# Two pairs of heads in one run of products with V, the compressed branch in the same run, gate rows through DRAM, and earlier loads of the compression weights

## The chip, the core and the metric

The kernel runs on one core of one Trainium2 chip. The metric is the device time of one execution in microseconds (us), as the median of several runs.

## The reference, cut to what is computed

Two transformer blocks of two layers each (DEPTH 2) act one after the other on x of 256 tokens by 1024. In the first block a context stream of another 256 tokens runs beside x in layer 0. Each of its layers, cut:

```
px = split_cols(hx @ w_in);  pc = split_cols(hc @ w_in)
ya, yca = global_gqa(...)             # 8 heads, "A"
yb, ycb = neighbourhood_attn(...)     # 8 heads, "B"
yc_, ycc = window_gqa(...)            # 8 heads, "C"
ux = concat([ya, yb, yc_]) * silu(px[9])
x = x + gate[:, None, :] * (ux @ w_out)
if need_ctx:                          # layer 0 alone
    uc = concat([yca, ycb, ycc]) * silu(pc[9])
    cx = cx + gate_c * (uc @ w_out)
```

`gate` and `gate_c` are rows of 1024 numbers, the last third of `c_silu @ ada_w + ada_b`. Each layer of the second block, cut:

```
x = x + 0.5 * swiglu(rms(x, ffn1_norm), ffn1_wg, ffn1_wu, ffn1_wd)
y_a = nsa(...) @ w_branch_nsa         # compressed + selected + window, 8 heads, "N"
y_b = moba(...) @ w_branch_moba       # 8 heads, "M"
x = x + (sigmoid(ga) * y_a + sigmoid(gb) * y_b) @ w_out
x = x + 0.5 * swiglu(rms(x, ffn2_norm), ffn2_wg, ffn2_wu, ffn2_wd)
```

In `nsa` the keys and values are also compressed (a two-layer net with weights w1 and w2 over blocks of 32 tokens), and each query attends to those few compressed keys too (`o_cmp = p_cmp @ vcb`); the three results are added with a gate per head.

## The kernel before

All large weights lie in one packed DRAM array and come in as tiles of up to 128x1024 f32 on SP's queue (`ws`, `_dma`, L260), in the fixed order of a plan. Each is split for TensorE by a cast on ScalarE into `wh` (L286) and a subtraction on VectorE into `wl` (L287), two tiles ahead of its use. `gemm` makes three products for each block of rows (`three`, L426 to L428: hi·hi, hi·lo, lo·hi) and adds them in a bank of PSUM (`acc`).

Beside the gemms run lanes: Python generators for the preparation of Q, K and V and for attention. After each block of gemm products `q()` gives the lanes a budget of time and `step()` takes the next step of the lane that lies furthest back. So the order of the program is that of Python; a scheduling layer then sets the order on each engine by what is ready.

`attention` handles units (a head, or half of one) of one or two slots. In each slot: scores (`f_s`, L514 and L515), softmax (`f_m`, L550; `f_n`, L566 to L574), transposes by TensorE of the normalised weights (`f_t`, L580, bank `pst`), a copy out (`f_e`, L596 or L598) to a tile `pt` in SBUF, of which there are three. `f_v` (L609) makes the products with V for two units: the stationary V is 64 columns wide, one unit fills the upper 64 partitions of the bank `pso`, the other the lower. A product of f32 operands shows in the trace as two records, called passes below. `evac` then adds the bank to its place (L985, L988) or splits it (L1398, L1412). `f_v` comes as soon as both units have ended one slot earlier. In the heads N a closure `extra` (L1374) adds the compressed branch to the bank: products 128 columns wide whose operands `Vb` and `pcT` fill 64 partitions.

At the end of a layer of block 1 the lanes are drained and the attention pools closed (L1097, L1098); then `gate` (tile `gt`) takes their space. For each stream and half row, four products with a broadcast column of `mod` and the identity (L1116) put the gate row on all partitions in a bank `psx`, and VectorE copies it (L1117). `w_out` runs on; `add` multiplies its banks by `gt` (`tmp`, L1123) and adds to x (L1124). In layer 0 the tile x had been overwritten by its normalised form at the start and then used for silu(gate) columns, so x and ctx are loaded again at L1110; `uc`, the context's input of `w_out`, is split at L1107 and L1108.

In block 2 the attention stage `mix` begins (L1205, L1218) by loading w1 (two tiles of 128x16x128, 1 MB each, in packets of 512 bytes) and w2 on ScalarE's queue, into tiles `big0`, `big1` and `w2` of the stage's own pools.

Of the kernel before, what the change touches and what calls it, by code (L numbers as in the profile page):

```python
# [228 lines left out]
class Body:  # L229
# [272 lines left out]
    def attention(self, units, evac):  # L502
# [97 lines left out]
        def f_v(x):  # L600
            pair = units[x:x + 2]
            O = self.ps("o")[:, :2 * P]
            extra = pair[1].get("extra")
            nk = len(pair[0]["v"])
            for k in range(nk):
                for i in (1, 0):
                    u = pair[i]
                    v, b, m, c = u["v"][k]
                    nc.tensor.matmul(O[HD * i:HD * i + HD, c:c + m * P], v, u["pt"][:, b:b + m, :].rearrange("p m t -> p (m t)"),  # L609
                                     start=k == 0, stop=k == nk - 1 and extra is None)  # L610
            if extra is not None:
                extra(O)
            evac(O, pair[1])

# [12 lines left out]
        for s in range(n):  # L627
# [11 lines left out]
            while nv < len(units) and ends[nv + 1] < s:  # L639
                f_v(nv)  # L640
                c += 430 * len(units[nv]["v"])
                nv += 2
            yield c
        while nv < len(units):
            f_v(nv)
            nv += 2
            yield 430.0
# [108 lines left out]
    def ada_close(self, g):  # L756
# [12 lines left out]
        while b < nb:  # L769
# [4 lines left out]
            for s in range(2):  # L774
# [5 lines left out]
                if a < z:  # L780
                    nc.vector.scalar_tensor_tensor(self.mod[l][:, s, a:z], self.mod[l][:, s, a:z], 1.0,
                                                   self.col("norm_w", 8 * l + a - 8, z - a), op0=ALU.add, op1=ALU.mult)
            b = e

# [35 lines left out]
    def block1(self, x):  # L820
        nc, tc = self.nc, self.tc
        cx = self.cx1
        with ExitStack() as es:
            hp = es.enter_context(tc.tile_pool(reuse_waits="tile", name="hT", bufs=1))
            hT = self.new_hT(hp, 0)
            with tc.tile_pool(reuse_waits="tile", name="w0", bufs=START_TILES) as self.w0:
                self.start(x, cx, hT)
# [5 lines left out]
    def start(self, x, cx, hT):  # L833
# [9 lines left out]
        self.norm_rows(x, x)  # L843
        self.norm_rows(cx, cx)

        def half(h):
            for c in (4 * h, 4 * h + 2):
                for s, v in enumerate((x, cx)):
                    self.mod_pair(0, s, c, self.turn_pair(v, c), hT)
# [31 lines left out]
    def layer1(self, l, x, cx, hT, hp):  # L881
# [3 lines left out]
        with ExitStack() as lay:  # L885
            lp = lay.enter_context(tc.tile_pool(reuse_waits="tile", name=f"lay{l}", bufs=1))
            if need:
                sg2 = lp.tile([P, 4, T], F32, name="sg2")
                xv, cv = (t.rearrange("p t (a d) -> p (t a) d", d=T) for t in (x, self.cx1))

                def sg(c, n):
                    return (xv, cv, sg2)[c // 4][:, c % 4:c % 4 + n, :]
# [17 lines left out]
            sink = lp.tile([P, 8], F32, name=f"sink{l}")  # L910
# [719 lines left out]
```

## Time and profile before

| quantity | value |
|---|---|
| device time, 3 runs | 1947.4 us median (1946.05 to 1948.95) |
| the profiled execution | 1947.63 us, its span 1945.8 us |
| TensorE (PE) | 1904.4 us busy, 98% of the span; granted clock 0.992 in the mean |
| VectorE (DVE) / ScalarE (ACT) / GpSimd (POOL) | 1279.4 us (66%) / 1103.3 us (57%) / 1.0 us |
| the chain that ended last | 92% PE, of which 72% gemm products (L426 to L428), 4% products with V, 4% transposes |
| DMA | 294.62 MB, 151 GB/s in the mean |

In the rows below a line of the timeline reads: start and length in us, engine, source line, operation, output and input tiles, shape, count. What stands in square brackets is how long the engine was idle before, and what ended that. Passes overlap, so what one costs is the distance of its start to the next start. PEclk in the windows is the granted clock as a share of full speed.

### The profile page before, as it was taken

Reading aid. Unit: us, or ns where it says so; the run is one execution under the profiler, and the core shown is the slowest. Engines: PE = TensorE matmul, PEld = TensorE weight load, DVE = VectorE, ACT = ScalarE, POOL = GpSimd, SP = SyncE. Lnnn points to the kernel's source line nnn. Section 1 sums busy time; section 2 is a strip of 40 time slices with the busy share of each in tenths; the row PEclk is TensorE's granted clock in tenths of the full one; section 3 lists DMA queues with packets and bytes.
Section 4 is the critical chain, followed back from the end, with each engine's and each line's share of the span. In section 5 each row is a group of like instructions: output and inputs, shape, how many; then the busy total and the mean of one; then the engine's idle time right before and its main releaser. Section 6 shows DMA issues by size and latency. Waiting matters only on the chain.

```text
span 1945.8 us, 27694 instructions
## 1 busy us (share of the span) xinstructions
PE 1904.4 (98%) x10348; PEld 1561.0 (80%) x10348; DVE 1279.4 (66%) x2490; ACT 1103.3 (57%) x1979; POOL 1.0 (0%) x7
## 2 busy tenths in 40 slices
PE   8999999999999999999899999999999899999998
PEld 3777778777988877888788878888888788888886
DVE  5486856788596787555689575555555588675555
ACT  4367657775567675444467645445444458655443
POOL 0000000000000000000000000000000000000000
PEclk9999999999999999999999999999999999999999
DMA  7333324135422236554523565554555433456552
GB/s 304 106 123 130 118 90 150 55 131 186 136 93 95 85 109 216 184 184 141 166 93 125 164 215 198 183 191 173 193 186 173 144 106 101 152 180 234 186 181 74
DMA packets 85270, 294.62 MB, mean 151 GB/s; under 512 B 10000, under 2 KB 10384, under 8 KB 85136
## 3 DMA queue, kind: packets, MB, share of 16 engines
q1 hardware_dynamic: 80432, 283.39, 43.0%
q10 hardware_dynamic: 4704, 9.47, 1.5%
q8 instruction: 81, 1.33, 0.3%
q14 instruction: 53, 0.43, 0.1%
HBM read 291.77 MB, written 1.05 MB: 150 GB/s over the span
## 4 chain that ended last, share of the span: by engine, by line
PE 92%; DVE 4%; ACT 2%; issue 1%; ACTq 1%; DMA 1%; SPq 0%; DVEq 0%
PE acc L426 24%; PE acc L428 24%; PE acc L427 24%; PE pso L609 4%; PE pst L580 4%; PE pss L514 2%; PE pss L515 2%; PE psr L715 1%; DVE wl L287 1%; PE psx L1173 1%; ACT wh L286 1%; PE psr L721 1%; PE psm L747 1%; PE psm L1260 1%; PE acc L750 1%
## 5 line engine op out<-in xcount | busy, mean ns | idle before, releaser
L287 DVE TENSOR_TENSOR wl<-ws,wh 128x1024 fp32r<-128x1024 f32 (+2 forms) x538 | 638.1, 1188 | 478.8 <-ACT wh L286 476.0
L286 ACT CAST wh<-ws 128x1024 fp32r<-128x1024 f32 (+2 forms) x538 | 549.2, 1024 | 573.3 <-PE acc L428 503.3
L426 PE MATMUL acc<-wh,xt 128*128 128x512 f32 (+3 forms) x1120 | 419.6, 376 | 11.7 <-ACT wh L286 11.7
L427 PE MATMUL acc<-wl,xt 128*128 128x512 f32 (+3 forms) x1120 | 416.6, 372 | 0.0
L428 PE MATMUL acc<-wh,xt 128*128 128x512 f32 (+3 forms) x1120 | 416.4, 373 | 0.0
L426 PEld LDWEIGHTS acc<-wh,xt 128*128 128x128 f32 x1120 | 212.1, 190 | 44.9 <-ACT wh L286 12.9
L428 PEld LDWEIGHTS acc<-wh,xt 128*128 128x128 f32 x1120 | 211.8, 189 | 33.0 <-issue 0.7
L427 PEld LDWEIGHTS acc<-wl,xt 128*128 128x128 f32 x1120 | 212.7, 190 | 31.2 <-issue 0.3
L426 PE MATMUL acc<-wh,hT 128*128 128x384 f32 (+2 forms) x480 | 159.6, 333 | 0.1
L427 PE MATMUL acc<-wl,hT 128*128 128x384 f32 (+2 forms) x480 | 158.5, 330 | 0.0
L428 PE MATMUL acc<-wh,hT 128*128 128x384 f32 (+2 forms) x480 | 158.1, 329 | 0.0
L550 ACT ACTIVATE p<-pss,nm 128x512 f32<-128x512 f32 (+2 forms) x240 | 127.5, 539 | 20.3 <-DVE nm L546 5.1
L426 PE MATMUL acc<-wh,hffn 128*128 128x512 f32 x352 | 137.7, 391 | 0.0
L428 PE MATMUL acc<-wh,hffn 128*128 128x512 f32 x352 | 137.1, 389 | 0.0
L427 PE MATMUL acc<-wl,hffn 128*128 128x512 f32 x352 | 137.0, 389 | 0.0
L580 PE MATMUL pst<-consts,p 128*128 128x128 f32 x624 | 103.3, 278 | 0.0
L427 PEld LDWEIGHTS acc<-wl,hT 128*128 128x128 f32 x480 | 90.6, 189 | 7.2 <-issue 1.9
L426 PEld LDWEIGHTS acc<-wh,hT 128*128 128x128 f32 x480 | 90.5, 189 | 6.8 <-issue 0.8
L428 PEld LDWEIGHTS acc<-wh,hT 128*128 128x128 f32 x480 | 90.5, 189 | 5.8 <-issue 1.2
L580 PEld LDWEIGHTS pst<-consts,p 128*128 128x128 f32 x624 | 72.2, 140 | 28.5 <-ACT p L572 5.6
L572 ACT ACTIVATE p<-p,rinv 128x256 f32<-128x256 f32 (+2 forms) x152 | 81.5, 573 | 16.5 <-DVE rinv L566 12.2
L428 PEld LDWEIGHTS acc<-wh,hffn 128*128 128x128 f32 x352 | 66.1, 188 | 13.9
(318 smaller groups left out, 2868.5 us busy)
## 6 DMA issues: line engine op xcount, KB each, us to landing
ws<-in_wall SPq DMA_DIRECT2D x476, 512.0 KB, 3.4
ws<-in_wall SPq DMA_DIRECT2D x64, 384.0 KB, 3.1
bias<-in_bias ACTq DMA_DIRECT2D x8, 512.0 KB, 4.0
x<-in_x SPq DMA_DIRECT2D x2, 1024.0 KB, 6.5
cx<-in_ctx SPq DMA_DIRECT2D x2, 1024.0 KB, 10.3
ws<-in_wall SPq DMA_DIRECT2D x4, 420.0 KB, 3.0
out<-y SPq DMA_DIRECT2D x2, 512.0 KB, 2.6
ws<-in_wall SPq DMA_DIRECT2D x2, 280.0 KB, 2.8
```

What stands on the lines that cost most here:

```text
L286: self.nc.scalar.copy(h[:, :n], s[:, :n])
L287: self.nc.vector.tensor_tensor(lo[:, :n], s[:, :n], h[:, :n].bitcast(F32), op=ALU.subtract)
L426: mm(out, ah, bh, start=start, stop=False)
L427: mm(out, ah, bl, start=False, stop=False)
L428: mm(out, al, bh, start=False, stop=stop)
L514: nc.tensor.matmul(S[:, o:o + w], q, kh, start=True, stop=False)
L515: nc.tensor.matmul(S[:, o:o + w], q, kl, start=False, stop=True)
L550: nc.scalar.activation(p[:, o:o + w], S[:, o:o + w], AF.Exp, bias=nm[:, i:i + 1], accum_out=sm[:, i:i + 1])
L572: nc.scalar.activation(p[:, o:o + w], p[:, o:o + w], AF.Copy, scale=r[:, i:i + 1])
L580: nc.tensor.transpose(t[:, i * P:(i + 1) * P], sl["P"][:, o:o + P], self.ident)
L609: nc.tensor.matmul(O[HD * i:HD * i + HD, c:c + m * P], v, u["pt"][:, b:b + m, :].rearrange("p m t -> p (m t)"), start=k == 0, stop=k == nk ...
L715: nc.tensor.transpose(p[:, 2 * a + g, :], ks[:, t, a, g, :], self.ident_r)
```

## The change

Six edits:

1. `f_v(x, n)` takes n = 2 pairs (four units): their products form one run, and both results lie in one bank, 256 columns each. In the loop it is called when all four units have ended a slot earlier, once per slot; what is left follows after the last slot. There are five `pt` tiles.
2. The compressed branch becomes products 64 columns wide in that same run: `extra` is now a list of four, `Vb` and `pcT` fill 128 partitions, the tile `scmp` is padded to eight rows with zeros by GpSimd.
3. x stays in its tile: the first norm writes to `xn0`, silu(gate) columns have a tile `sg0`, and only ctx is loaded again.
4. The gate rows go through DRAM: when `mod` is finished, GpSimd's queue writes its gate columns to a DRAM tile (`gate_rows`), and at the end of the layer one broadcast DMA per stream, on ScalarE's queue, reads the row into `gt` (L1126 of the new kernel). The 24 products and 6 copies are gone.
5. `cmp_load`: w1 and w2 are issued in the second round of `ffn1` instead of at the start of `mix`, into tiles of a pool that lasts through block 2.
6. The last norm's weight is loaded one stage later; the sink values share one tile.

```diff
-                u["pt"] = self.pp.tile([P, 8, P], F32, tag="pt", name=f"pt_{self.uid}", bufs=3)
+                u["pt"] = self.pp.tile([P, 8, P], F32, tag="pt", name=f"pt_{self.uid}", bufs=5)
...
+        def f_v(x, n):
+            pairs = [(units[x + 2 * j], units[x + 2 * j + 1], 2 * P * j) for j in range(n)]
+            O = self.ps("o")
+            todo = []
+            for pair in pairs[::-1]:
+                for k in range(len(pair[0]["v"])):
+                    for i in (1, 0):
+                        v, b, m, c = pair[i]["v"][k]
+                        todo.append((i, c + pair[2], m * P, v, pair[i]["pt"][:, b:b + m, :].rearrange("p m t -> p (m t)")))
+            for pair in pairs[::-1]:
+                todo += [(i, c + pair[2], P, v, p) for i, c, v, p in pair[1].get("extra", [])]
+            for y, (i, c, w, v, p) in enumerate(todo):
+                nc.tensor.matmul(O[HD * i:HD * i + HD, c:c + w], v, p, start=y < 2, stop=y >= len(todo) - 2)
+            for pair in pairs:
+                evac(O[:, pair[2]:pair[2] + 2 * P], pair[1])
...
-            while nv < len(units) and ends[nv + 1] < s:
-                f_v(nv)
-                c += 430 * len(units[nv]["v"])
-                nv += 2
+            if nv + 3 < len(units) and ends[nv + 3] < s:
+                f_v(nv, 2)
+                c += 860 * len(units[nv]["v"])
+                nv += 4
...
+    def gate_rows(self, l, c0, n):
+        if l not in self.gates:
+            self.gates[l] = self.gp.tile([2, KD, P], F32, name=f"gates{l}")
+        c = c0 // P
+        for s in range(2 if l == 0 else 1):
+            self.nc.gpsimd.dma_start(self.gates[l][s, c:c + n // P, :].rearrange("j p -> p j"), self.mod[l][:, s, 16 + c:16 + c + n // P])
...
-                    for t, nm in ((x, "x"), (cx, "ctx")):
-                        nc.sync.dma_start(t, self.dram[nm].rearrange("o (t p) d -> p (o t) d", p=P))
+                    nc.sync.dma_start(cx, self.dram["ctx"].rearrange("o (t p) d -> p (o t) d", p=P))
                 for s in range(2 if need else 1):
-                    for ct in range(2):
-                        p = self.ps("x")
-                        for j in range(4):
-                            g = self.mod[l][:, s, 16 + 4 * ct + j:17 + 4 * ct + j]
-                            nc.tensor.matmul(p[:, j * P:(j + 1) * P], g.to_broadcast([P, P]), self.ident, start=True, stop=True)
-                        nc.vector.tensor_copy(gate[:, s, ct * 512:ct * 512 + 512], p)
+                    g = self.gates[l][s:s + 1].rearrange("s j p -> s (j p)")
+                    nc.scalar.dma_start(gate[:, s, :], g.to_broadcast([P, D]))
...
+    def cmp_load(self, l):
+        nc = self.nc
+        w1 = [self.bp.tile([P, 16, P], F32, tag=f"big{j}", name=f"w1{l}_{j}") for j in range(2)]
+        for j, nm in enumerate(("cmpk_w1_2", "cmpv_w1_2")):
+            nc.scalar.dma_start(w1[j], self.dram[nm][l].rearrange("(m p) j -> p m j", p=P))
...
+                if fi == 1 and name == "ffn1":
+                    self.cmp_load(l)
...
-                            def extra(O, t=t, b=b, pcT=pcT):
-                                for j in range(2):
-                                    nc.tensor.matmul(O[:, j * P:(j + 1) * P], Vb[:, b, 2 * j:2 * j + 2, :].rearrange("p r d -> p (r d)"),
-                                                     pcT[:, t, :], start=False, stop=j == 1)
+                            extra = [(i, j * P, Vb[:, b, 2 * j + i, :], pcT[:, t, :]) for j in range(2) for i in (1, 0)]
...
-            if i == 1:
+            if i == 2:
                 fw = bp.tile([P, D], F32, tag="xtrow", name="fw2")
```

**First place: TensorE, last runs of the heads A in layer 0.** Before, the two pairs have a run each (L609), with transposes and gemm products between them (`pso` is the bank of V's products, `pst` that of transposes, `pss` scores):

```order
1497 L580 MATMUL pst_3666<-consts,p_3597 128x128 x4
1498 L609 MATMUL pso_3678<-pt_3654,VG_584 64x256
1499 L609 MATMUL pso_3678<-pt_3593,VG_584 64x256
1500 L609 MATMUL pso_3678<-pt_3654,VG_584 64x256
1501 L609 MATMUL pso_3678<-pt_3593,VG_584 64x256
1502 L514 MATMUL pss_3750<-KTB_587,QTB_589 128x512
...
1514 L428 MATMUL acc_3690<-wh_3522,hT_1_109 128x384
1515 L609 MATMUL pso_3719<-pt_3717,VG_584 64x256
1516 L609 MATMUL pso_3719<-pt_3676,VG_584 64x256
1517 L609 MATMUL pso_3719<-pt_3717,VG_584 64x256
1518 L609 MATMUL pso_3719<-pt_3676,VG_584 64x256
1519 L580 MATMUL pst_3764<-consts,p_3744 128x128 x4
```

In the change the same eight products (L612) are one run in one bank:

```order
1525 L426 MATMUL acc_3692<-wh_3694,hT_0_110 128x384
1526 L612 MATMUL pso_3719<-pt_3717,VG_592 64x256
1527 L612 MATMUL pso_3719<-pt_3682,VG_592 64x256
1528 L612 MATMUL pso_3719<-pt_3717,VG_592 64x256
1529 L612 MATMUL pso_3719<-pt_3682,VG_592 64x256
1530 L612 MATMUL pso_3719<-pt_3660,VG_592 64x256
1531 L612 MATMUL pso_3719<-pt_3560,VG_592 64x256
1532 L612 MATMUL pso_3719<-pt_3660,VG_592 64x256
1533 L612 MATMUL pso_3719<-pt_3560,VG_592 64x256
1534 L580 MATMUL pst_3757<-consts,p_3737 128x128 x4
```

Over the whole program TensorE's order has 66 unbroken stretches of L609 and 10 of L1374 before, and 37 stretches of L612 now; the products in them are 320 and 16 before and 352 now.

**Second place: ScalarE at the start of the first `mix`, and where its loads stand now.** Before, the three loads stand between two casts of weight tiles:

```order
875 L286 CAST wh_9954<-ws_9886 128x840
876 L1205 DMA w_0_10014<-in_cmpk_w_2 128x16x128
877 L1205 DMA w_1_10015<-in_cmpv_w_2 128x16x128
878 L1218 DMA w_10034<-in_cols 128x128
879 L286 CAST wh_10038<-ws_9904 128x560
```

In the change they stand at the end of layer 1 of block 1, spread among casts, with that layer's gate row (`gt`, L1126) between them:

```order
754 L286 CAST wh_8332<-ws_8244 128x1024
755 L1160 DMA w_0_8787<-in_cmpk_w_2 128x16x128
756 L979 CAST u_0_7957<-cx_84 128x256
757 L1126 DMA gt_8329<-gates_2520 128x1024
758 L286 CAST wh_8350<-ws_8262 128x1024
759 L1160 DMA w_1_8788<-in_cmpv_w_2 128x16x128
760 L286 CAST wh_8397<-ws_8280 128x1024
```

The two w1 tiles of the second `mix` stand in the `w_out` of the first, two casts apart.

**Third place: VectorE at the end of layer 0 of block 1.** Before, a copy of a gate row (L1117) stands ahead of the first `tmp` (L1123):

```order
726 L1117 COPY gt_4740<-psx_4782 128x512
727 L287 TENSOR_TENSOR wl_4813<-ws_4477,wh_4812 128x1024
728 L1117 COPY gt_4740<-psx_4788 128x512
729 L1123 TENSOR_TENSOR tmp_4741<-acc_4141,gt_4740 128x512
730 L1123 TENSOR_TENSOR tmp_4741<-acc_4142,gt_4740 128x512
731 L1124 TENSOR_TENSOR x<-x,tmp_4741 128x512 x2
732 L287 TENSOR_TENSOR wl_4835<-ws_4540,wh_4834 128x1024
```

In the change the first `tmp` (L1132) follows the last subtraction of `uc` (L1122), and two tiles' `wl` stand behind it:

```order
713 L1122 TENSOR_TENSOR uc_4744<-cx_84,uc_4743 128x256
714 L1132 TENSOR_TENSOR tmp_4742<-acc_4244,gt_4741 128x512
715 L1132 TENSOR_TENSOR tmp_4742<-acc_4245,gt_4741 128x512
716 L287 TENSOR_TENSOR wl_4791<-ws_4537,wh_4790 128x1024
717 L1133 TENSOR_TENSOR x<-x,tmp_4742 128x512 x2
718 L287 TENSOR_TENSOR wl_4813<-ws_4623,wh_4812 128x1024
```

On ScalarE both broadcasts of that layer's gate rows stand directly behind the last cast of `uc` (L1121) and ahead of the cast to wh_4790.

## Rows read from the trace of the kernel before

**Rows 1.** The page's chain that ended last, by engine.

```profile
PE 92%; DVE 4%; ACT 2%; issue 1%; ACTq 1%; DMA 1%; SPq 0%; DVEq 0%
```

**Rows 2.** PE's timeline, heads A of layer 0: start us, length us, engine, line, operation.

```profile
342.50 1.08 PE L609 MATMUL pso<-pt,VG 128*64 128x256 f32 x8
343.51 0.66 PE L580 MATMUL pst<-consts,p 128*128 128x128 f32 x4
```

**Rows 3.** PE's timeline, end of layer 1 of block 1.

```profile
733.36 0.40 PE L426 MATMUL acc<-wh,u 128*128 128x512 f32 x1
733.68 1.95 PE L609 MATMUL pso<-pt,VB 128*64 128x256 f32 x16
735.56 0.50 PE L427 MATMUL acc<-wl,u 128*128 128x512 f32 x1
735.90 0.40 PE L428 MATMUL acc<-wh,u 128*128 128x512 f32 x1
736.14 0.40 PE L426 MATMUL acc<-wh,u 128*128 128x512 f32 x1
...
737.53 1.95 PE L1116 MATMUL psx<-consts,mod 128*128 128x128 f32 x16
739.24 0.47 PE L426 MATMUL acc<-wh,u 128*128 128x512 f32 x1
```

**Rows 4.** PE's timeline in the first mix: a run of heads M, the compressed products of heads N.

```profile
992.11 0.87 PE L609 MATMUL pso<-pt,mVY 128*64 128x256 f32 x8
...
1015.80 0.49 PE L1374 MATMUL pso<-pcT,Vb 64*128 64x128 f32 x2
1016.22 0.44 PE L580 MATMUL pst<-consts,p 128*128 128x128 f32 x2
```

**Rows 5.** ACT's timeline at the start of the first mix.

```profile
940.17 0.85 ACTq L1205 DMA_DIRECT2D w<-in_cmpk_w  x1
...
944.59 3.41 ACTq L1218 DMA_DIRECT2D w<-in_cols  x1
948.12 1.39 ACT L286 CAST wh<-ws 128x560 fp32r<-128x560 f32 x2 [6.67 <-issue]
```

**Rows 6.** PE's timeline, the first product after the loads, in the first and the second mix.

```profile
949.56 0.69 PE L426 MATMUL acc<-wh,xt 128*128 128x384 f32 x1 [4.97 <-ACT wh L286]
...
1542.27 0.97 PE L426 MATMUL acc<-wh,xt 128*128 128x384 f32 x2 [5.14 <-ACT wh L286]
```

**Rows 7.** Windows (us, busy us of PE, PEld, DVE, ACT, POOL with instructions, PEclk, DMA share, GB/s).

```profile
1340.00:1350.00 10.00, 9.71 (x44) 7.76 (x44) 7.59 (x19) 4.56 (x8) 0.00 (x0) 1.00 0.70 255
949.50:956.00 6.50, 6.44 (x32) 5.97 (x33) 5.58 (x21) 4.22 (x11) 0.00 (x0) 0.70 0.56 175
1542.00:1550.00 8.00, 7.73 (x36) 7.28 (x37) 6.40 (x22) 5.17 (x13) 0.00 (x0) 0.67 0.47 140
```

**Rows 8.** DMA issues of the whole run: queue, count, KB each, median us from issue to landing.

```profile
fw<-in_final_norm_w SPq DMA_DIRECT2D x1, 512.0 KB, 4.2
fw<-in_final_norm ACTq DMA_DIRECT2D x1, 512.0 KB, 7.1
w<-in_cols ACTq DMA_DIRECT2D x2, 64.0 KB, 7.1
```

**Rows 9.** DVE's timeline at the ends of the two layers of block 1.

```profile
449.59 1.28 DVE L1123 TENSOR_TENSOR tmp<-acc,gt 128x512 f32<-128x512 f32 x2
...
744.56 1.28 DVE L1123 TENSOR_TENSOR tmp<-acc,gt 128x512 f32<-128x512 f32 x2
```

**Rows 10.** ACT's timeline at the same two ends: the last cast of uc, the last of u.

```profile
443.34 0.40 ACT L1107 CAST uc<-cx 128x256 fp32r<-128x256 f32 x1
...
736.14 0.41 ACT L965 CAST u<-cx 128x256 fp32r<-128x256 f32 x1 [2.77 <-DVE cx L988]
```

**Rows 11.** PE's timeline at the end of layer 0, its last run with V.

```profile
440.83 0.82 PE L609 MATMUL pso<-pt,VB 128*64 128x256 f32 x6
441.58 0.50 PE L426 MATMUL acc<-wh,u 128*128 128x512 f32 x1
```

More of the change, by code (lines that the diff above doesn't have):

```diff
@@ L598, in f_e @@
                 nc.vector.tensor_copy(dst, src)
[L600 to L613, printed above, removed]
+        def f_v(x, n):
[13 more added lines that the diff above has]
+                evac(O[:, pair[2]:pair[2] + 2 * P], pair[1])
         ends, e = [], -1
@@ L825, in block1 @@
             hT = self.new_hT(hp, 0)
-            with tc.tile_pool(reuse_waits="tile", name="w0", bufs=START_TILES) as self.w0:
-                self.start(x, cx, hT)
+            with tc.tile_pool(reuse_waits="tile", name="w0", bufs=START_TILES) as self.w0, \
+                    tc.tile_pool(reuse_waits="tile", name="xn0", bufs=1) as xp:
+                self.start(x, cx, hT, xp)
             for l in range(DEPTH):
@@ L831, in block1, with start @@
                 hT = self.layer1(l, x, cx, hT, hp)
-    def start(self, x, cx, hT):
+    def start(self, x, cx, hT, xp):
         nc, tc = self.nc, self.tc
@@ L842, in start @@
         nc.vector.tensor_copy(self.ident_r, self.ident)
-        self.norm_rows(x, x)
-        self.norm_rows(cx, cx)
+        xn, cn = (xp.tile([P, 2, D], F32, name=f"xn0_{j}") for j in range(2))
+        self.norm_rows(x, xn)
+        self.norm_rows(cx, cn)
         def half(h):
             for c in (4 * h, 4 * h + 2):
-                for s, v in enumerate((x, cx)):
+                for s, v in enumerate((xn, cn)):
                     self.mod_pair(0, s, c, self.turn_pair(v, c), hT)
@@ L887, in layer1 @@
             if need:
-                sg2 = lp.tile([P, 4, T], F32, name="sg2")
-                xv, cv = (t.rearrange("p t (a d) -> p (t a) d", d=T) for t in (x, self.cx1))
+                sgs = [lp.tile([P, 4, T], F32, name="sg0"), cx.rearrange("p t (a d) -> p (t a) d", d=T),
+                       lp.tile([P, 4, T], F32, name="sg2")]
                 def sg(c, n):
-                    return (xv, cv, sg2)[c // 4][:, c % 4:c % 4 + n, :]
+                    return sgs[c // 4][:, c % 4:c % 4 + n, :]
             else:
@@ L909, in layer1 @@
             qn = lp.tile([P, 2, HD], F32, name=f"qn{l}")
-            sink = lp.tile([P, 8], F32, name=f"sink{l}")
+            sinks = lp.tile([P, 64], F32, name=f"sink{l}")
+            sink, nsink = sinks[:, :8], sinks[:, 8:16]
             nc.scalar.dma_start(qn[:, 0, :], self.row_bcast(self.dram["k_norm_a"], l * HD, HD))
@@ L913, in layer1 @@
             nc.scalar.dma_start(sink, self.row_bcast(self.dram["sink_c"], l * 8, 8))
-            nsink = lp.tile([P, 8], F32, name=f"nsink{l}")
             nc.vector.tensor_scalar(nsink, sink, -1.0, None, op0=ALU.mult)
@@ L1143, in layer1 @@
                 return hT
+    def cmp_load(self, l):
[3 more added lines that the diff above has]
+            nc.scalar.dma_start(w1[j], self.dram[nm][l].rearrange("(m p) j -> p m j", p=P))
+        w2 = self.bp.tile([P, 2, HD], F32, tag="w2", name=f"w2{l}")
+        o2 = COLS["w2"][0] + P * l
+        nc.scalar.dma_start(w2, self.dram["cols"][:, o2:o2 + P].rearrange("p (a d) -> p a d", a=2))
+        self.cmp_w = w1, w2
     def ffn(self, l, name, x, xt, ss, hooks, after):
@@ L1202, in mix @@
             toks = [(0, None), (1, None)]
-            w1 = [op.tile([P, 16, P], F32, tag=f"big{j}", name=f"w1{l}_{j}") for j in range(2)]
-            for j, nm in enumerate(("cmpk_w1_2", "cmpv_w1_2")):
-                nc.scalar.dma_start(w1[j], self.dram[nm][l].rearrange("(m p) j -> p m j", p=P))
+            w1, w2 = self.cmp_w
             oT = {k: [op.tile([P, 4, 256], F32R, name=f"o{k}{l}_{j}") for j in range(2)] for k in "NM"}
@@ L1349, in attn_lane @@
                         yield 2000.0
-                        sc = mp.tile([P, 2, 4, 16], F32, tag="scmp", name=f"scmp{l}{b}")
+                        scp = mp.tile([P, 2, 8, 16], F32, tag="scmp", name=f"scmp{l}{b}")
+                        nc.gpsimd.memset(scp, 0.0)
+                        sc = scp[:, :, :4, :]
                         st = mp.tile([P, 2, 4], F32, tag="stc", name=f"stc{l}{b}")
```

34 lines of the change are left out of this document (18 added, 16 removed).

## The prediction

> **What bounds the kernel now.** I read the chain that ended last first: 92% of the span is PE's own work [rows 1]. So nothing is won by relieving DVE or ACT; time goes only where PE has less to do, or where it stood idle or slow. Then I went through PE's timeline for two things. One is the distance from start to start around the runs with V [rows 2 to 4], which shows what such a run costs beyond its passes. The other is brackets with idle time: the two largest of the whole run are at the starts of the two mixes [rows 6], and ACT's timeline at that place says why [rows 5]. The windows give the clock there [rows 7]. Last, for the gate rows, which turn from PE work into a transfer, I read how long transfers of this size take [rows 8] and when the row is wanted [rows 9 to 11].
>
> **The sum** is made against the profiled execution, 1947.6 us, 0.2 above the median of the runs. 0.2% is about 4 us, what a measurement of this kernel can tell from no change.
>
> *Fewer runs with V: -8.7.* Sixteen passes take 1.88 us from their start to the next product's (733.68 to 735.56) [rows 3], eight take 1.01 (342.50 to 343.51) [rows 2]. So eight more passes cost 0.87, 0.109 each, and 1.01 - 0.87 = 0.14 is fixed in each run. The product ahead of the run takes 0.32 instead of 0.24 (733.36 to 733.68; 735.90 to 736.14 is an undisturbed one), the one behind it 0.34 instead of 0.24 [rows 3]. A run thus costs 0.14 + 0.08 + 0.10 = 0.32 beyond its passes. PE's order has 66 such runs before and 37 after, 29 fewer. Where transposes follow the run the price behind it is not in these rows, so the lower bound is 0.22 each (6.4 us), the upper 0.32 (9.3). I take 0.30, near the upper, since gemm products follow most runs: 29 x 0.30 = 8.7.
>
> *Compressed branch: -2.0.* Its 10 stretches go. Two passes take 0.42 (1015.80 to 1016.22) [rows 4]; the 128-row gate passes take 0.107 each (1.71 for sixteen, 737.53 to 739.24) [rows 3], so two would take 0.21 undisturbed: 0.2 x 10 = 2.0. The passes themselves come out even: 32 before at 0.107 are 3.4; after, 64 passes of half the width and 128 columns. A run of eight of which four are 128 columns long is 0.87 against 1.08 long [rows 4, 2], so such a pass is 0.05 cheaper than 0.109, about 0.056, and 64 are 3.6. If they cost 0.107 after all, it would be 3.4 us more.
>
> *Gate products: -5.3.* 24 products, 48 passes at 0.107 to 0.12: 5.1 to 5.8, two thirds of it in layer 0. The six copies on DVE cost nothing before as far as PE goes, and give nothing, save that in layer 0 they stood ahead of `tmp`.
>
> *Starts of the mixes: -13.* At the first, ACT is held by three DMA issues from 940.17 to about 948.0 [rows 5]; the casts of the next weight tiles stand behind them, so PE idles 4.97 us, at the second mix 5.14 [rows 6]. Then PE works at a granted clock of 0.70 for 6.5 us and 0.67 for 8.0 us, against 1.00 at the start of another stage [rows 7]: 6.5 x 0.30 + 8.0 x 0.33 = 4.6. With an estimated 1.5 us for smaller gaps and a lowered clock around the stall, that is 10.1 + 4.6 + 1.5 = 16.2. An ordinary stage start is not free: PE is busy 9.71 of 10.00 us there [rows 7], 0.6 lost in twenty us at the least; I leave 1.6 at each start. So 16.2 - 2 x 1.6 = 13. Bounds: 10 (only the idle goes) and 16.
>
> Where do the issues go? In the new order they stand at the end of layer 1 of block 1, and in the first mix's `w_out`, with casts between them. The first issue took 0.85 us, the third 3.41 [rows 5], with nothing between: the queue took them no faster than it drained. With casts between, each has some us to drain, and ACT runs two tiles ahead of PE. I price the new places at 0, covered by that lead; if the cover is gone, rival B.
>
> *Gate rows as transfers: +8.* The order puts the reads of layer 0 behind the last cast of `uc`. Before, the last run with V ended at 441.6 [rows 11] and that cast at 443.7 [rows 10]. The 512 KB broadcasts of the trace land after 4.2 and 7.1 us [rows 8], so the row is there 6.3 to 9.2 us after the run, with two of them at once rather later; before, `tmp` came 8.0 us after it (449.59) [rows 9]. But PE has less to do in the meantime. Behind the last run stand 31 gemm products (0.23 each, 7.1 us) until PE needs a bank that `tmp` frees, and two `wl` stand behind `tmp` on DVE. So PE idles between 0 and 4 us; I take 3.5, as the second read shares the engines with the first. In layer 1 the read stands behind the cast of `u` (736.14, ending 0.98 us after the run's end at 735.56) [rows 10, 3] and behind the first w1 tile. PE wants the row about 6.6 us after the run, before it was used 9.0 after (744.56) [rows 9]; it lands 1.0 + 4.2 at best, 1.0 + 10 behind a megabyte: 0 to 4.4, I take 3. Both waits can lower the clock for some us as the mix starts do [rows 7]; at half of that price, 1.5. Together 8, bounds 0 and 13.
>
> The Trainium skill, "DMA: Bandwidth & Descriptors", section "Queues, rings and completion order", speaks against this part: descriptors of one issuing queue are consumed in ring order on each DMA engine, so a gate row behind w1 on ScalarE's queue starts last. The trace agrees: 64 KB behind the w1 tiles took 7.1 us, as long as 512 KB elsewhere [rows 8]. By the rule alone the wait in layer 1 would be at its upper bound, the sum 1.4 us worse. The same page, section "Anatomy of one DMA", fits 2.0 us and 436 KB per us on GpSimd's queue, 3.2 us for 512 KB; no row here is that short, and by it the sum would be some 3 us better.
>
> *Without a price.* x is not loaded again: nothing in the rows waits for that load. GpSimd's memsets and the writes of `mod` are done long before they are read. Five `pt` tiles take away waits, none of which is on the chain by more than tenths.
>
> Sum: -8.7 - 2.0 - 5.3 - 13 + 8 = -21: 1926.6, less the 0.2: **1926.5 us**.
>
> **Rivals.**
> *A, the gate rows are in time.* They land at the lower bounds, and nothing is given back: 1926.5 - 8 = 1918.5. For it: 4.2 us [rows 8]. Against it: on ACT's queue the same size took 7.1.
> *B, the block on ACT's queue only moves.* The queue drains 2 MB no faster elsewhere; at the end of layer 1 and in `w_out` ACT is held again by some 7 us, casts come late, and PE idles about 5 us twice with the slow clock behind it: the 13 are given back, 1939.5. For it: from the first issue's start to the last one's end it was 7.8 us [rows 5]. Against it: casts stand between them now.
> *C, slower: the joined run is no longer there to fill a gap.* Before, each slot's softmax had a run of about 1.0 us [rows 2] between its transposes and the next; now every second slot has none, and PE waits for the softmax chain wherever no gemm product is ready. 29 such gaps at 1.0 are +29: 1955.5. It decides from 21 of the 29 on, which eats the whole gain. For it: attention leaves few gemm products at the ends of the layers. Against it: in the order gemm products stand between most slots.
>
> **How the numbers follow.** Forecast 0.52, A 0.20, B 0.20, C 0.08. The forecast's own range is 1921 to 1933. The range to 1912 takes in A with the upper price of the runs and of the mix starts, to 1941 B; what lies outside is C and a little of B and A. Faster by over 0.2% are the forecast, A and most of B: 0.89. Within 0.2%: B with the gate waits at their upper bound and the mild end of C, 0.04. Slower: the rest of C, 0.07.
>
> **What would show it.** In the new profile: 37 runs of L612 and eight passes more costing 0.87; no idle of about 5 us in brackets at a mix start, and a clock near 1.00 in the 15 us after it; on ACT, DMA issues under 1 us each at the new places; PE idle 2 to 4 us ahead of a product that waits for `tmp` at the end of each layer of block 1. It is wrong if PE's idle ahead of transposes and of V's products grows by over 10 us in sum (C), if a bracket of 4 us or more follows the new places of L1160 (B), or if `tmp` never waits (A).

## The result and the profile after

The change runs in 1922.0 us (median of 4, 1921.4 to 1924.0), beside 1946.8 of the kernel before: a ratio of 0.9873, with a 95% interval from 0.9856 to 0.989. That is 24.8 us less, where 20.9 less were forecast; 1922.0 lies in the range.

The page of the change: span, engines, and the chain that ended last.

```profile
span 1920.2 us, 27632 instructions
PE 1882.2 (98%) x10332; PEld 1552.8 (81%) x10332; DVE 1272.8 (66%) x2484; ACT 1102.6 (57%) x1979; POOL 4.9 (0%) x14
...
PE 89%; DVE 6%; DMA 2%; ACT 2%; issue 1%; SPq 0%; ACTq 0%; DVEq 0%
```

PE still bounds it; ACT's queue, 1% of the chain in [rows 1], is at 0%, and DVE and DMA have more of it. The lines that the page names for those two are `wl` (L287, 2%, before 1%) and the weight tiles `ws` (1%), not the new transfers; where these are waited for is read from the timelines below.

**Runs with V.** PE's timeline of the change at the end of layer 0: what stood there before as three runs (the last in [rows 11]) is one.

```profile
431.83 0.39 PE L426 MATMUL acc<-wh,u 128*128 128x512 f32 x1
432.15 2.81 PE L612 MATMUL pso<-pt,VB 128*64 128x256 f32 x24
434.89 0.50 PE L427 MATMUL acc<-wl,u 128*128 128x512 f32 x1
```

24 passes take 2.74 us from start to start. At 0.109 each that leaves 0.12, about the 0.14 fixed cost that eight [rows 2] and sixteen [rows 3] gave. The product ahead takes 0.32 (432.15 - 431.83), as in [rows 3]. In the first mix the compressed products follow as part of the run:

```profile
1009.30 2.81 PE L612 MATMUL pso<-pt,mVX 128*64 128x256 f32 x24
1011.94 1.04 PE L612 MATMUL pso<-pcT,Vb 128*64 128x128 f32 x16
1012.91 0.45 PE L426 MATMUL acc<-wh,xt 128*128 128x384 f32 x1
```

Sixteen of them take 0.97, 0.061 each (0.056 was the estimate).

**Start of the first mix.** ACT's timeline, then the windows of the change there. Where ACT was held for 6.67 us [rows 5], casts follow one another at their usual distance; PE is busy 24.55 of 25 us at a granted clock of 1.00, against 0.70 in [rows 7].

```profile
928.35 0.90 ACT L286 CAST wh<-ws 128x840 fp32r<-128x840 f32 x1 [1.82 <-PE acc L428]
931.07 0.66 ACT L286 CAST wh<-ws 128x560 fp32r<-128x560 f32 x1 [1.82 <-PE acc L428]
```

```profile
920.00:945.00 25.00, 24.55 (x138) 21.62 (x137) 15.92 (x34) 14.10 (x22) 0.40 (x2) 1.00 0.45 127
```

**The loads at their new place**, and the gate row of layer 1 between them (ACT's timeline of the change):

```profile
724.89 0.84 ACTq L1160 DMA_DIRECT2D w<-in_cmpk_w  x1
728.82 0.41 ACT L979 CAST u<-cx 128x256 fp32r<-128x256 f32 x1 [2.94 <-DVE cx L1002]
728.91 0.34 ACTq L1126 DMA_DIRECT2D gt<-gates  x1
730.17 1.05 ACT L286 CAST wh<-ws 128x1024 fp32r<-128x1024 f32 x1 [0.95 <-PE acc L428]
...
730.24 0.72 ACTq L1160 DMA_DIRECT2D w<-in_cmpv_w  x1
```

The second w1 tile takes 0.72 to issue, not 3.07 as back to back, and no cast is late.

**The gate rows.** Layer 0 in ACT's and then DVE's timeline of the change: the first read is issued at 435.88, with nine casts of `uc` still to come that stand ahead of it in the order. It lands 4.1 us later, at 440.0, just as DVE is through with `uc`. `tmp` follows without a gap. Behind it PE has one gap of 0.99 us, at 457.29 ahead of L812; the kernel before has 0.42 there. With the same transfers e2 has none above 0.3 and e3 0.30, so it is not put down to the gate rows.

```profile
435.78 0.40 ACT L1121 CAST uc<-cx 128x256 fp32r<-128x256 f32 x1
435.88 0.34 ACTq L1126 DMA_DIRECT2D gt<-gates  x1
...
438.54 0.40 ACT L1121 CAST uc<-cx 128x256 fp32r<-128x256 f32 x1
```

```profile
439.70 0.42 DVE L1122 TENSOR_TENSOR uc<-cx,uc 128x256 fp32r<-128x256 f32 x1
440.10 1.29 DVE L1132 TENSOR_TENSOR tmp<-acc,gt 128x512 f32<-128x512 f32 x2
```

Layer 1: the row lands 6.6 us after its issue, DVE waits 3.15 us for it, and PE has three gaps behind that, 4.0 us, where the kernel before had one of 1.69. DVE's timeline, then PE's:

```profile
735.63 1.29 DVE L1132 TENSOR_TENSOR tmp<-acc,gt 128x512 f32<-128x512 f32 x2 [3.15 <-DMA gt<-gates]
```

```profile
737.57 0.44 PE L467 MATMUL psx<-consts,x 128*128 128x128 f32 x2 [1.30 <-DVE x L1133]
742.46 0.41 PE L467 MATMUL psx<-consts,x 128*128 128x128 f32 x2 [1.58 <-DVE x L1133]
745.84 0.87 PE L467 MATMUL psx<-consts,x 128*128 128x128 f32 x6 [1.13 <-DVE x L1133]
```

### The profile page after: what moved, and what is told of

It reads as the page before. It is cut to its first block, busy times and chain, and to the rows that moved or that the text cites. A ratio compares the mean times of both kernels' runs of the same rounds, so it can differ in the third digit from the quotient of the medians.

```text
span 1920.2 us, 27632 instructions
## 1 busy us (share of the span) xinstructions
PE 1882.2 (98%) x10332; PEld 1552.8 (81%) x10332; DVE 1272.8 (66%) x2484; ACT 1102.6 (57%) x1979; POOL 4.9 (0%) x14
## 4 chain that ended last, share of the span: by engine, by line
PE 89%; DVE 6%; DMA 2%; ACT 2%; issue 1%; SPq 0%; ACTq 0%; DVEq 0%
PE acc L426 24%; PE acc L428 23%; PE acc L427 23%; PE pso L612 4%; PE pst L580 4%; PE pss L514 2%; PE pss L515 2%; DVE wl L287 2%; DMA ws<-in_wall 1%; PE psr L717 1%; PE psx L1195 1%; PE psr L723 1%; ACT wh L286 1%; PE psm L1277 1%; PE acc L752 1%
## 5 line engine op out<-in xcount | busy, mean ns | idle before, releaser
L287 DVE TENSOR_TENSOR wl<-ws,wh 128x1024 fp32r<-128x1024 f32 (+2 forms) x538 | 637.7, 1187 | 455.5 <-ACT wh L286 452.7
L427 PE MATMUL acc<-wl,xt 128*128 128x512 f32 (+3 forms) x1120 | 415.2, 371 | 1.4 <-DVE wl L287 1.4
L427 PEld LDWEIGHTS acc<-wl,xt 128*128 128x128 f32 x1120 | 211.0, 188 | 34.1 <-DVE wl L287 2.9
L427 PE MATMUL acc<-wl,hT 128*128 128x384 f32 (+2 forms) x480 | 158.6, 330 | 0.0
L427 PE MATMUL acc<-wl,hffn 128*128 128x512 f32 x352 | 137.0, 389 | 0.0
L427 PEld LDWEIGHTS acc<-wl,hT 128*128 128x128 f32 x480 | 90.7, 189 | 5.5 <-issue 0.4
```

The lines of the kernel that those rows point to most:

```text
L287: self.nc.vector.tensor_tensor(lo[:, :n], s[:, :n], h[:, :n].bitcast(F32), op=ALU.subtract)
L427: mm(out, ah, bl, start=False, stop=False)
```

## The experiments

The times of one kernel scatter by up to some 0.4% between lowest and highest (e8: 1942.1 to 1949.4), and a part of that lies in the first 125 us: in the thirteen profiles the 31st subtraction of a weight tile (L287) starts between 121.6 and 126.2 us, with no order by edit. The granted clock from 20 to 121.5 us is 0.93 in the two that are latest (e4, e7) and 1.00 in e1 alone. So beside the ratio of times each experiment has its *inner* time: from the start of the 31st to the start of the 531st of the 538 subtractions in its profile. It is 1786.4 for the kernel before, and 1761.8 and 1762.2 in two profiles of the change: 24.4 less. All other kernels have one profile each, so an inner time is that of one execution.

| kernel | median, us | ratio to before, 95% interval | inner time | against |
|---|---|---|---|---|
| the change, first / again | 1922.0 / 1922.9 | 0.9873 [0.9856, 0.989] / 0.9879 [0.9864, 0.9895] | 1761.8 / 1762.2 | before: -24.4 |
| e1, gates by PE | 1921.9 | 0.9876 [0.9862, 0.9889] | 1765.0 | change: +3.0 |
| e2, gate row of layer 1 early | 1919.8 | 0.9865 [0.985, 0.988] | 1760.0 | change: -2.0 |
| e3, loads in the mix | 1931.7 | 0.9926 [0.9914, 0.9939] | 1772.2 | change: +10.2 |
| e6, single pairs | 1929.8 | 0.9913 [0.9899, 0.9926] | 1768.7 | change: +6.7 |
| e4, early loads alone | 1934.1 | 0.9939 [0.9927, 0.9952] | 1773.1 | before: -13.3 |
| e5, loads by GpSimd | 1935.2 | 0.9951 [0.9938, 0.9963] | 1775.8 | before: -10.6 |
| e7, gate rows alone | 1946.6 | 1.0002 [0.9993, 1.001] | 1787.2 | before: +0.8 |
| e8, gate rows and x kept | 1944.1 | 0.9993 [0.9983, 1.0002] | 1784.1 | before: -2.3 |
| e10, x kept alone | 1947.3 | 1.0005 [0.9997, 1.0014] | 1788.0 | before: +1.6 |
| e9, x loaded again | 1928.5 | 0.9912 [0.9896, 0.9928] | 1766.5 | change: +4.5 |

### The starts of the mixes

**e3: the change with the loads' tiles in the mix's own pools.**

```diff
-        w1 = [self.bp.tile([P, 16, P], F32, tag=f"big{j}", name=f"w1{l}_{j}") for j in range(2)]
+        w1 = [op.tile([P, 16, P], F32, tag=f"big{j}", name=f"w1{l}_{j}") for j in range(2)]
...
-                if fi == 1 and name == "ffn1":
-                    self.cmp_load(l)
...
+            self.cmp_load(l, op, mp)
             w1, w2 = self.cmp_w
```

> The change with w1 and w2 in tiles of the mix stage's own pools again, so that the three loads stand back to back at the start of each mix. Theory 1: the held queue of ScalarE is what the earlier loads removed; PE idles about 5 us at both starts, at a clock of about 0.7 behind it: 1922 + 13 = 1935. Theory 2: the starts would be good without it, since x is kept and runs are joined: under 1926. Besides: the gate row of layer 1 has no w1 tile ahead of it here. If the queue's order delayed it (6.6 us to landing in the change, 4.1 and 4.9 in layer 0), it lands after 4 to 5 us here; if not, after 6.6.

Theory 1 holds. ACT's and PE's timelines of e3 show the hold and the gap of before again:

```profile
927.74 3.51 ACTq L1160 DMA_DIRECT2D w<-in_cmpv_w  x1
931.29 3.73 ACTq L1163 DMA_DIRECT2D w<-in_cols  x1
935.12 1.39 ACT L286 CAST wh<-ws 128x560 fp32r<-128x560 f32 x2 [7.41 <-issue]
```

```profile
936.57 0.97 PE L426 MATMUL acc<-wh,xt 128*128 128x384 f32 x2 [5.71 <-ACT wh L286]
...
1527.31 0.97 PE L426 MATMUL acc<-wh,xt 128*128 128x384 f32 x2 [4.52 <-ACT wh L286]
```

The granted clock behind the first is 0.69 for 10 us. Between the subtractions on both sides of the starts it takes 7.2 and 6.0 us more than the change (7.22 and 6.04), 13.3, as forecast. Its time is only 9.2 above the change (1922.4, the mean of its two medians) because layer 1 gains: the gate row, with no w1 tile ahead of it, lands after 5.0 us and not 6.6, and PE's gaps there fall from 4.0 to 2.3 us.

The edit moves the call and the pool of the tiles together; which of the two sets the place of the loads is not shown.

**e4: before with that edit alone** (w1, w2 and graw from the lasting pool, `cmp_load` in `ffn1`).

```diff
-            w1 = [op.tile([P, 16, P], F32, tag=f"big{j}", name=f"w1{l}_{j}") for j in range(2)]
-            for j, nm in enumerate(("cmpk_w1_2", "cmpv_w1_2")):
-                nc.scalar.dma_start(w1[j], self.dram[nm][l].rearrange("(m p) j -> p m j", p=P))
+            w1, w2 = self.cmp_w
...
+                if fi == 1 and name == "ffn1":
+                    self.cmp_load(l)
```

> The kernel before with one edit of the change: w1 and w2 lie in tiles of the pool that lasts through block 2, so that their loads stand spread at the end of layer 1 and in the first mix's w_out. Theory 1: the starts of the mixes are worth 13 us, and the new places cost nothing where no gate row stands behind w1: 1946.5 - 13 = 1933.5. Theory 2 (the forecast's rival B, in part): the loads hold ScalarE's queue in the new places too, and 3 us or more come back: above 1936.5.

Theory 1 again: 12.3 us less in time, 13.3 in the inner time, 6.1 and 6.8 of it at the two starts. The new places cost nothing.

**e5: before with the three loads issued by GpSimd, at the old place.**

```diff
-                nc.scalar.dma_start(w1[j], self.dram[nm][l].rearrange("(m p) j -> p m j", p=P))
+                nc.gpsimd.dma_start(w1[j], self.dram[nm][l].rearrange("(m p) j -> p m j", p=P))
...
-            nc.scalar.dma_start(w2, self.dram["cols"][:, o2:o2 + P].rearrange("p (a d) -> p a d", a=2))
+            nc.gpsimd.dma_start(w2, self.dram["cols"][:, o2:o2 + P].rearrange("p (a d) -> p a d", a=2))
```

> The kernel before with one edit: the three loads at the start of each mix are issued on GpSimd's queue instead of ScalarE's, at the same place in the program. Theory 1: what stalled PE there is ScalarE's queue, held by the issues, so its casts came late; with the issues elsewhere the idle time of 5 us and the slow clock behind it go: 1946.5 - 13 = 1933.5. Theory 2: the 2 MB of loads compete with the weight tiles on the DMA engines, and the casts would wait for tiles anyway: the brackets stay near 5 us, released by a DMA, and the time is 1946.

It separates the held engine from the transfers. The 2 MB move at the start of the mix as before, the DMA engines are full in that window (share 1.01), and PE is hardly touched at the first start (windows, then PE's largest gap there, of e5). The last line is the largest gap at the second:

```profile
940.00:950.00 10.00, 9.33 (x63) 8.61 (x62) 7.65 (x23) 6.36 (x11) 1.13 (x3) 1.00 1.01 306
```

```profile
943.84 0.44 PE L427 MATMUL acc<-wl,xt 128*128 128x384 f32 x1 [0.67 <-DVE wl L287]
...
1543.70 0.63 PE L1241 MATMUL psm<-consts,kd 128*128 128x128 f32 x4 [1.65 <-DVE Z L1244]
```

So theory 1: ACT's held queue was the stall. One changed word per load is worth 11.2 us in time. The earlier loads of e4 are worth somewhat more in the inner time, 13.3 against 10.6. Most of that lies at the second start, where e5 gains 4.9 and e4 6.8; the 1.65 us ahead of L1241 are not in e4. The intervals of the ratios overlap.

### The runs with V

**e6: the change with one pair in each run.**

```diff
-            if nv + 3 < len(units) and ends[nv + 3] < s:
-                f_v(nv, 2)
-                c += 860 * len(units[nv]["v"])
-                nv += 4
+            while nv < len(units) and ends[nv + 1] < s:
+                f_v(nv, 1)
+                c += 430 * len(units[nv]["v"])
+                nv += 2
...
-            m = min(2, (len(units) - nv) // 2)
+            m = 1
```

> The change with f_v for one pair each time; the compressed products stay in the run of their pair, five pt tiles stay. PE's order has 71 runs of L612 instead of 37. Theory 1: each run costs 0.30 us beyond its passes: 1922 + 34 x 0.30 = 1932. Theory 2 (the forecast's rival C): joined runs leave gaps in the softmax that single runs fill, so part of the gain is lost and undoing costs less than 5: under 1927.

The result lies between: 7.3 us above the change (1922.4), 6.7 in the inner time. Undoing costs, so rival C did not eat the gain. But 6.7 / 34 = 0.20 is not the price of a run, because e6 also waits less. From the 31st to the 166th subtraction lie layers 0 and 1 of block 1. PE's windows there, of the kernel before, the change and e6 (length, PE busy, PEclk, DMA share, GB/s):

```profile
124.38:774.41 650.03, 644.51 (x4018) 1.00 0.35 119
123.26:765.14 641.88, 632.04 (x3971) 1.00 0.40 125
123.13:769.92 646.79, 639.61 (x3970) 1.00 0.39 124
```

e6 has 51 runs here, the change 25. PE is busy 7.57 us longer, 0.29 for each of the 26: the 0.30 of the forecast. But it idles 7.18 us in e6 and 9.84 in the change, so 2.7 of it do not show. Two places make the difference. One is the gate row of layer 1, with one gap of 1.10 in e6 where the change has three, 4.0 in sum. The other is heads C of layer 0, where the change has two gaps that e6 lacks (PE's timeline of the change; the largest of e6 in these heads are 0.46 and 0.48; the run of [rows 2] is from heads C too, not A):

```profile
381.25 0.50 PE L514 MATMUL pss<-KTG,QTG 128*128 128x512 f32 x1 [1.02 <-ACT p L550]
...
394.19 0.66 PE L580 MATMUL pst<-consts,p 128*128 128x128 f32 x4 [0.73 <-ACT pt L596]
```

PE waits there for the softmax and for the copy behind the transposes: rival C, in small. At the end of layer 0 it is the other way round, 1.84 us ahead of L427 in e6, 0.99 ahead of L812 in the change.

In each mix e6 takes 1.0 us more than the change, with ten unbroken stretches of V's and compressed products against six. The kernel before takes 0.7 more than e6 in each, and has ten stretches there too (six of its ten compressed ones stand right beside a run). So the 0.7 is the compressed branch inside the stretches, not their number. Together the mixes behind their starts take 3.4 us less in the change than before.

### The gate rows and x

**e1: the change with gates by PE** (the old block of L1112 to L1117 in place of the DMA, and no writes of `mod`).

```diff
-                    g = self.gates[l][s:s + 1].rearrange("s j p -> s (j p)")
-                    nc.scalar.dma_start(gate[:, s, :], g.to_broadcast([P, D]))
+                    for ct in range(2):
+                        p = self.ps("x")
+                        for j in range(4):
+                            g = self.mod[l][:, s, 16 + 4 * ct + j:17 + 4 * ct + j]
+                            nc.tensor.matmul(p[:, j * P:(j + 1) * P], g.to_broadcast([P, P]), self.ident, start=True, stop=True)
+                        nc.vector.tensor_copy(gate[:, s, ct * 512:ct * 512 + 512], p)
```

> The changed kernel with its gate rows made by TensorE again (24 products L1116 and 6 copies of the kernel before), all else as in the change. Theory 1: the transfers cost little. In the profile of the change the gate row of layer 1 leaves PE idle 1.30, 1.58 and 1.13 us ahead of L467 at 737 to 746, against 1.69 at the same place before, so 2.3 us are given back of the 5.3 that the products cost. Undoing the edit then gives 1922 + 3 = 1925, and the three brackets shrink to one of about 1.7. Theory 2 (the forecast's term): the waits cost 8 in all, and undoing gives 1922 - 2.7 = 1919.

In times it cannot be told from the change, so neither number came. In the inner time undoing costs 3.0, theory 1's value: 2.4 to 2.6 at the end of layer 0, 0.3 to 0.7 in layer 1, where the three gaps shrink to one of 1.88. Behind that gap e1's granted clock is 0.66 from 743.8 to 748.8, at 1.00 in the change and in the kernel before (gap 1.69). e2 has the same 0.66 behind a gap of 1.93, and there PE is busy 0.9 us longer than the change from the 116th to the 166th subtraction, with the same products; so about 1.0 of the 3.0, an estimate from that, is the clock of e1 and not the gate rows.

The start was 1.5 to 2.4 us shorter in e1's profile. Kernels with the writes of `mod` have starts from 121.6 to 126.2 and those without from 121.7 to 124.8, so I put it down to scatter; that the writes cost something there is not excluded. The profiled run is also the slowest of e1's four (1923.4; the others 1921.0 to 1922.3), so the 3.0 is not certain.

**e7: before with the gate rows alone through DRAM** (the two edits to `mod` and `gate` of the change).

> The kernel before with one edit of the change: the gate rows go through DRAM. No w1 tile stands ahead of the gate row of layer 1 here. Theory 1: PE saves 5.3 us of products and gets no new wait, since the row of layer 0 is issued while uc is still being cast and the row of layer 1 lands in 4 to 5 us: 1946.5 - 5 = 1941.5. Theory 2 (the forecast's term): the waits cost 8: 1946.5 + 2.7 = 1949.

Neither theory as it was put: the time is that of before, and the trace says why. DVE's timeline and PE's largest gap at the end of layer 0:

```profile
449.10 1.29 DVE L1129 TENSOR_TENSOR tmp<-acc,gt 128x512 f32<-128x512 f32 x2
453.13 1.29 DVE L1130 TENSOR_TENSOR x<-x,tmp 128x512 f32<-128x512 f32 x2 [2.75 <-DMA x<-in_x]
454.34 2.35 DVE L287 TENSOR_TENSOR wl<-ws,wh 128x1024 fp32r<-128x1024 f32 x2
```

```profile
455.62 0.79 PE L427 MATMUL acc<-wl,uc 128*128 128x512 f32 x1 [4.25 <-DVE wl L287]
```

The gate row is in time (`tmp` has no bracket). It is x, on its way back from DRAM, that the addition waits for; two `wl` stand behind it on DVE, and PE runs dry, at a clock of 0.85 in the next 20 us. Layer 1, with no w1 tile ahead, gains 2.0 in the inner time.

**e8: e7 with x kept; e10: before with x kept alone; e9: the change with x loaded again.** The edit of e8 and e10 is that of the change to `start` and `sg`, with

```diff
-                    for t, nm in ((x, "x"), (cx, "ctx")):
-                        nc.sync.dma_start(t, self.dram[nm].rearrange("o (t p) d -> p (o t) d", p=P))
+                    nc.sync.dma_start(cx, self.dram["ctx"].rearrange("o (t p) d -> p (o t) d", p=P))
```

and e9 takes it back in the change.

> The kernel before with two edits of the change: gate rows through DRAM, and x kept in its tile. With the gate rows alone the time was that of before, and the trace showed why: at the end of layer 0 the addition to x waited 2.75 us for x to come back from DRAM, two wl tiles stood behind it on DVE, and PE idled 4.25 us. Theory 1: the two edits need each other; with x kept that bracket goes and the 5.3 us of products show: 1946.4 - 5 = 1941.5. Theory 2: the bracket was the gate row's after all, and stays: 1946.

> The kernel before with x kept alone; the gate rows are TensorE's products. Theory 1: in the kernel before x was back by the time the addition wanted it, because the gate products and copies came first; keeping x gives nothing: 1946.4, within 1.5. Theory 2: the load of x cost something that the brackets don't show (its place on SP's queue, bandwidth): 1944 or less.

> The change with x overwritten at the start and loaded again at the end of layer 0, as before; all else as in the change. Theory 1: the addition to x on DVE (L1133 in the change, at 442.4) waits for the load, wl behind it is late, and PE idles some us there, with a lower clock behind it: 1922.4 + 3 to 6 = 1925 to 1928. Theory 2: x kept is worth nothing here either: 1922.

Alone, keeping x gives nothing (e10, theory 1). Its inner time is 1.6 up: 0.8 in layer 0, where PE waits 0.90 us ahead of L427 at 452.88 (before 0.22), and 0.4 at the start of each mix. In the change taking it away costs 6.1 us in time, 4.5 in the inner time (e9, theory 1), and the same bracket appears. DVE's and PE's timelines of e9:

```profile
445.13 1.29 DVE L1132 TENSOR_TENSOR x<-x,tmp 128x512 f32<-128x512 f32 x2 [2.56 <-DMA x<-in_x]
```

```profile
447.61 0.65 PE L427 MATMUL acc<-wl,uc 128*128 128x512 f32 x1 [3.94 <-DVE wl L287]
```

e8 is a half hit: the gap falls from 4.25 to 1.83 us, the inner time by 3.1 against e7, but the time is 1944.1, not 1941.5, and its interval takes in no change. What is left of the gap is `uc` and `tmp` themselves on DVE, with 0.34 of waiting for the gate row:

```profile
451.64 0.50 PE L427 MATMUL acc<-wl,uc 128*128 128x512 f32 x1 [1.83 <-DVE wl L287]
```

e6, the change with single pairs, has 1.84 at the same place; with joined runs the gap is gone.

**e2: the change with the gate row of layer 1 read early, into a tile of its own.**

```diff
+            if not need:
+                gate1 = lp.tile([P, 1, D], F32, name="gt1e")
+                nc.scalar.dma_start(gate1[:, 0, :], self.gates[l][0:1].rearrange("s j p -> s (j p)").to_broadcast([P, D]))
...
-                gate = wp.tile([P, 2, D], F32, name=f"gt{l}")
+                gate = wp.tile([P, 2, D], F32, name=f"gt{l}") if need else gate1
...
-                for s in range(2 if need else 1):
+                for s in range(2 if need else 0):
```

> The change with one edit: the gate row of layer 1 has a tile of its own in the layer's pool and is read at the start of the layer, some 270 us ahead of its use. Theory 1: what the change gave back in layer 1 is the late landing of this row (its tile takes the space of the attention pools, and it stands behind the first w1 tile on ScalarE's queue). The 4.0 us of brackets ahead of L467 at 737 to 746 fall to the 1.7 of the kernel before or less: 1922 - 2.3 = 1919.7. Theory 2: the brackets come from DVE, whose order there has tmp and x behind wl; then they stay, and the time is 1922.

Theory 1: the three gaps become one of 1.93, near the 1.69 of the kernel before, and the time is 1919.8, the lowest of all. PE's timeline of e2:

```profile
739.92 0.41 PE L467 MATMUL psx<-consts,x 128*128 128x128 f32 x2 [1.93 <-DVE x L1136]
```

Its interval overlaps that of the change, so by times alone the 2 us are not certain. In the inner time they are there (-2.0), but only some 1.2 to 1.6 lie in layer 1: of the 2.1 us of gaps, 0.9 are lost to the lower clock behind the one gap that is left. The rest is the gap of 0.99 ahead of L812 at the end of layer 0, which is under 0.3 in e2; the edit was not meant to touch it.

### The change again

> The change itself once more, on the same chip as these three, to compare them with. Both theories: 1922, ratio 0.987. Its profile is also a second look at the brackets ahead of L467 in layer 1 (4.0 us in the first) and at the landing of the gate rows: if the queue's order delays the row of layer 1, it is again the slowest of the three.

1922.9, ratio 0.9879. The gaps ahead of L467 are 4.3 us, and the row of layer 1 is again the slowest to land (the view of its line, L1126, for all three rows):

```profile
DMA to landing us min/median/max: 4.2/5.0/6.9
```

## Why the prediction was right, point by point

The time, 1922.0, lies 4.5 us below the forecast, in the range and near the lower end of the forecast's own (1921). The work that was to go went as forecast; the waits that were to come were sized too high. By subtractions, the inner time of the first profile (24.7 less than before) splits in three: the two starts of the mixes 13.1, where 13 stood; the mixes behind them 3.4, where four runs at 0.30 and 2.0 for the compressed branch make 3.2; layers 0 and 1 of block 1 8.2, where 25 runs at 0.30, 5.3 for the gate products and 8 of waits make 4.8. In those layers PE is busy 12.5 us less (forecast 12.8) and idles 4.3 more (forecast 8). So the one large miss is the waits, and in it two misses work against each other: the gate rows gave back some 5 us less than forecast, heads C 1.3 more.

- *Starts of the mixes, -13*: right in place, mechanism and size. 13.3 by e3 and by e4; e5 shows that it is ACT's queue and not the traffic. That the new places are covered held too: the second w1 tile took 0.72 to issue, and rival B did not come.
- *Compressed branch, -2.0*: the 3.4 of the mixes, less four runs at 0.25 to 0.30, leave 2.2 to 2.4. A pass of half width took 0.061.
- *Fewer runs with V, -8.7*: right in mechanism and in price. By e6 a run costs PE 0.29 of busy time in layers 0 and 1 (26 runs) and 0.25 in the mixes (four in each); the fixed part held (0.12 at 24 passes), and so did 0.32 for the product ahead. What the term put at nothing is the idle time that the joined runs leave in heads C of layer 0, 1.02 and 0.73 us, where the kernel before has one gap of 0.44: 1.3 us, which rival C had named and priced at 29.
- *Gate products, -5.3, and their transfers, +8*: the products held (what is left of the 12.5 after 25 runs at 0.29 is 5.2), the transfers did not. The forecast had the pair lose 2.7. By the inner time of e1 it gains 3.0, some 1.0 of that e1's lower clock; by times the two cannot be told apart. Of the waits, layer 0 had 0 at `tmp` where 3.5 stood: the step that failed is that the read would be issued after the last cast of `uc`, 2.1 us after the run's end. It went 1.0 us after it, ahead of casts that stand before it in the order. The 4.1 us to landing then fit under the 5.1 that DVE takes from the addition to `cx` to the end of `uc` (435.01 to 440.12). Layer 1 had 2.3 (4.0 of gaps against 1.69) where 3 stood, by the mechanism named: 6.6 us behind a w1 tile, 5.0 without one in e3. The 1.5 for a lowered clock did not come; the gaps are 1.1 to 1.6 us long each, and the granted clock is 1.00 in the window from 707 to 753.

The forecast also held against rival A that "on ACT's queue the same size took 7.1". The same view of the kernel before has eight more loads of 512 KB on that queue, tiles of `bias` and not broadcasts, and they landed sooner:

```profile
bias<-in_bias ACTq DMA_DIRECT2D x8, 512.0 KB, 4.0
```

The part "without a price" was wrong in one point that the sum did not show. "Nothing in the rows waits for that load" of x was true before, and e10 agrees; but once the gate products and copies are gone the addition comes early enough to wait for x, and keeping x is worth 4.5 to 6 us (e9). The gate rows without it are worth nothing (e7). The right question was the forecast's own: what is late next. The last step of the sum, 1926.6 less 0.2, is 1926.4 and not 1926.5; nothing hangs on it.

Rival A came true for layer 0 alone, B not, C by 1.3 us. The rule on the order within an issuing queue ("DMA: Bandwidth & Descriptors" in the Trainium skill, section "Queues, rings and completion order") named the right place: by it the row of layer 1 would start last. The trace agrees in kind (landings after 5.8 to 6.9 us behind a w1 tile in the change, the change again, e6 and e9; 4.9 to 5.5 without one in e3, e7 and e8), but the price was about 2 us at most and not the whole of a megabyte. The estimate of 3.2 us for 512 KB from the same page of the Trainium skill (section "Anatomy of one DMA", a fit for GpSimd's queue) is below every landing of a gate row seen here (3.9 at least, in e7); the shortest of the eight `bias` loads did take 3.2.

## What to carry to other kernels

Here three loads issued back to back, two of 1 MB in packets of 512 bytes, held ScalarE's queue for 8 us, and its casts with it; whether the size of the packets matters was not tried. Give such loads to an idle engine's queue, or to tiles that are free earlier, so that they spread (11 to 13 us here). When work is taken off the busy engine, ask which operand is the next to arrive late, and price the edits together: the gate rows alone and x kept alone gave nothing, and without x kept the whole change was 6 us slower. Before a difference of two times is divided by a count, ask what else changed: e6 gave 0.20 a run by its time and 0.29 by PE's busy time, because its waits were others. Where a transfer stands in an engine's order is not when it is issued; read that from the trace.

## What the runs showed of the hardware that was not expected

A DMA issue on ScalarE's queue goes ahead of compute instructions that stand before it on that engine and have not begun: the gate row's came at 435.88, nine casts of `uc` from before it in the order ran after it, the last at 438.54. The profiles of e2, e3, e9 and of the change again have the same nine, e6 and e8 four. The reverse was not seen: while the queue was held at the start of a mix, the cast behind waited for 6.67 us.

The hold ended when the first of the three loads had landed, not when all had. In the ten starts with the loads on ScalarE's queue (before, e3, e7, e8, e10) the third issue ended within 0.5 us of the first w1 tile's landing: at 948.0 and 948.1 in the first start before, while the second w1 tile landed at 951.6.

The same loads on GpSimd's queue, with the DMA engines as full (share 1.01 for 10 us), left PE with a largest gap of 0.67 us at the first start and of 1.65 at the second, where on ScalarE's queue it was 4.97 and 5.14.
